# Stick-breaking weights by summation by parts: running products used as they are, values replaced by their steps along the sequence

## The chip, the cores and the metric

The program runs on one NeuronCore of a Trainium2 chip. Its matrix engine is TensorE (PE in the profile, with its weight loads shown apart as PEld), beside it work VectorE (DVE), ScalarE (ACT), GpSimd (POOL) and SyncE (SP), which issues nearly all transfers. The engines run side by side and meet at semaphores. The metric is the device time of one execution of the whole program in microseconds (us), as a median of several runs.

## The reference

Two layers on an input of 1024 rows by 1024 columns, float32: an attention layer and a recurrent layer, each followed by a dense SwiGLU block, with norms around every part. The change lies in the attention layer alone. It has 8 heads of ordinary chunked softmax attention (group A) and 8 heads of stick-breaking attention (group B), 64 columns each:

```
z = einsum('bqhd,bkhd->bhqk', q_blk, k) * scale
causal = kpos[None, :] < qpos[:, None]
log_beta = log_sigmoid(z)
log_1m_beta = where(causal, log_sigmoid(-z), 0.0)
after = cumsum(log_1m_beta, axis=3, reverse=True) - log_1m_beta
w = where(causal, exp(log_beta + after), 0.0)
o = einsum('bhqk,bkhd->bqhd', w, v)
```

Without logarithms: with s(k) = sigmoid(-z(k)) for k before the query and 1 from there on, and R(k) the product of s from k to the end, the weight of key k is w(k) = R(k+1) - R(k). The output is the sum of w(k) v(k) over the keys. Summation by parts turns it into the sum of (1 - R(k)) (v(k) - v(k-1)), with v(-1) = 0: the same number from other factors.

## The kernel before

The heads are worked in pairs, in the order 4, 5, 6, 7, 0, 1, 2, 3: first the four stick-breaking ("sigmoid") pairs, then the four softmax pairs. For each pair, `project` (L311) multiplies the normed input with the pair's query and key weights on PE (two query tiles and two key tiles `psq`, each 24 matmuls, in two PSUM banks `proj` that take turns), and ACT and DVE bring the results to SBUF as high and low parts `st` (L326 to L335). The values of two pairs at a time are computed by `v_tile` (L281, tiles `psv` in the same two banks) and brought to SBUF by `evacuate` (L298) as `v`, one tile [128, 8, 128] for each pair: partition p and block t hold key 128 t + p.

`attend` (L338) then takes the 8 query blocks of 128 rows one after the other, and the two heads of the pair in each. For a sigmoid pair, query block i has n = 128 (i + 1) keys, and for each head:

- PE makes the scores `sc` (L389, L390); ACT takes the sigmoid into `pr` (L397); POOL sets the entries from the diagonal on to 1 (L408), and column n to 1 (L407);
- DVE makes the running product R from the right, in place, by a scan (L411), and then the weights as the difference of neighbours, in place (L415); for the last block it also clears the last column (L417);
- PE transposes `pr` in blocks of 128 (L427) into one of two PSUM banks `tr`; ACT copies up to 512 columns at a time to SBUF as `pt` (L431);
- PE multiplies `pt` with `v` into `pso` (L356). These value matmuls are held back and run in bursts, for sigmoid pairs after blocks 3, 5, 6 and 7.

Four `pr` buffers take turns, so a sigmoid of a later block waits until the transposes of an earlier one have run. The weights' high and low parts and some other tiles share a ring of eight buffers "w" (`split`, L142 to L158).

The order on each engine is fixed when the program is built: a list scheduler places all instructions of all stages by estimated times. While a pair is attended, the projections and value tiles of the next pair are placed between its instructions, so PE has other matmuls (`psq`, `psv`) between scores and transposes.

Of the kernel before, what the change touches and what calls it, by code (L numbers as in the profile page):

```python
# [8 lines left out]
F32 = mybir.dt.float32  # L9
F32R = mybir.dt.float32r  # L10
BF16 = mybir.dt.bfloat16
AF = mybir.ActivationFunctionType
ALU = mybir.AluOpType
PSUM = bass.MemoryType.PSUM

P = 128
S = 1024
# [3 lines left out]
NT = S // P  # L21
# [78 lines left out]
class Trunk:  # L100
# [164 lines left out]
    def attention(self, x_src, xT_src, w_v, w_qk, bias_t, o_dst, hT, pools, open_first):  # L265
        nc, tc = self.nc, self.tc
        with ExitStack() as ctx:
# [6 lines left out]
            def turned_bank():  # L274
                return self.pt.tile([P, 512], F32, tag="tr", bufs=2, name=self.uid("tr"))
# [22 lines left out]
            def evacuate(vt, t2, both=False):  # L298
                psv = psvs.pop(t2)
                for tt in range(2):  # L300
# [4 lines left out]
                        nc.scalar.activation(vt[0][:, t, :], psv[:, tt, 0, :], AF.Copy, scale=rsc[:, t:t + 1])  # L305
                    nc.scalar.activation(vt[1][:, t, :], psv[:, tt, 1, :], AF.Copy, scale=rsc[:, t:t + 1])

            def v_alloc():
                return [ap.tile([P, NT, P], F32, tag="v", bufs=3, name=self.uid("v")) for _ in range(2)]

            def project(p, ws=(None, None)):  # L311
                st = [[ap.tile([P, S], F32R, tag="st", bufs=12, name=self.uid("st"))
                       for _ in range(3)] for _ in range(2)]
                for which in range(2):
                    w = ws[which] or self.split(w_qk[p, which], KT, P)
                    for half in range(2):
                        ps = prp.tile([P, 512], F32, tag="proj", bufs=2, name=self.uid("psq"))
                        self.proj_T(ps, w, slice(0, P), hT, half)
                        cs = slice(half * HALF, (half + 1) * HALF)
                        if which or p < 4:  # L320
                            nc.vector.tensor_tensor(ps, ps, rsb[:, cs], op=ALU.mult)
                        for h in range(2):
                            own, oth = (slice(0, 64), slice(64, P)) if h == 0 else (slice(64, P), slice(0, 64))
                            qs, k1, k2 = st[h]
                            if which == 0:
                                nc.scalar.activation(qs[own, cs], ps[own, :], AF.Copy, scale=-0.125)  # L326
                                nc.vector.scalar_tensor_tensor(
                                    qs[oth, cs], ps[own, :], -0.125, qs[own, cs].bitcast(F32),
                                    op0=ALU.mult, op1=ALU.subtract)
                            else:  # L330
                                nc.scalar.copy(k1[own, cs], ps[own, :])
                                nc.scalar.copy(k1[oth, cs], ps[own, :])
                                nc.vector.tensor_tensor(k2[own, cs], ps[own, :], k1[own, cs].bitcast(F32),
                                                        op=ALU.subtract)
                                nc.vector.tensor_copy(k2[oth, cs], k2[own, cs].bitcast(F32))  # L335
                return st

            def attend(p, st, vt):  # L338
                bias = [None, None]
# [25 lines left out]
                for i in range(NT):  # L365
                    k0 = max(0, i - 4) if p < 4 else 0
                    nb = i + 1 - k0
                    n = nb * P
# [4 lines left out]
                    w = n // n_c  # L373
                    for h in range(2):
                        qs, k1, k2 = st[h]
                        q = qs[:, i * P:(i + 1) * P]
                        if p < 4 and h == 1:
                            pr = ap.tile([P, 640], F32, tag="nata", bufs=3, name=self.uid("pr"))
                        else:
                            pr = ap.tile([P, 1024], F32, tag="nat", bufs=4, name=self.uid("pr"))  # L380
                        if p < 4:
                            mn = ap.tile([P, 2], F32, tag="mn", bufs=4, name=self.uid("mn"))
                            mn = [mn[:, c:c + 1] for c in range(n_c)]
                            sm = ap.tile([P, 1], F32, tag="sm", bufs=4, name=self.uid("sm"))
                        for c in range(n_c):
                            sc = pp.tile([P, 512], F32, tag="sc", bufs=3, name=self.uid("sc"))[:, :w]
                            ks = slice(k0 * P + c * w, k0 * P + c * w + w)
                            cs = slice(c * w, c * w + w)
                            nc.tensor.matmul(sc, q, k1[:, ks], start=True, stop=False)  # L389
                            scored = nc.tensor.matmul(sc, q, k2[:, ks], start=False, stop=True).ins  # L390
                            if p < 4:
                                off = 640 - n + c * w
                                nc.vector.tensor_tensor_reduce(
                                    pr[:, cs], sc, bias[h][:, off:off + w], 1.0, 3e38,
                                    op0=ALU.add, op1=ALU.min, accum_out=mn[c])
                            else:
                                nc.scalar.activation(pr[:, cs], sc, AF.Sigmoid, scale=rsc[:, i:i + 1])  # L397
                        if p < 4:
                            if n_c == 2:
                                nc.vector.tensor_tensor(mn[0], mn[0], mn[1], op=ALU.min)  # L400
                            nc.scalar.activation(pr[:, :n], pr[:, :n], AF.Exp, bias=mn[0], scale=-1.0,
                                                 accum_out=sm)
                            nc.vector.reciprocal(sm, sm)
                            nc.gpsimd.tensor_scalar(pr[:, :n], pr[:, :n], sm, 1.0, op0=ALU.mult, op1=ALU.mult)
                        else:
                            if n < S:
                                nc.gpsimd.memset(pr[:, n:n + 1], 1.0)  # L407
                            nc.gpsimd.affine_select(pr[:, n - P:n], pr[:, n - P:n], pattern=[[-1, P]],  # L408
                                                    compare_op=ALU.is_gt, fill=1.0, base=0,
                                                    channel_multiplier=1)  # L410
                            nc.vector.tensor_tensor_scan(  # L411
                                pr[:, 0:n][:, ::-1], pr[:, 0:n][:, ::-1], self.zero.to_broadcast([P, n]),
                                1.0, op0=ALU.mult, op1=ALU.add)
                            m = n if n < S else n - 1
                            nc.vector.tensor_tensor(pr[:, 0:m], pr[:, 1:m + 1], pr[:, 0:m], op=ALU.subtract)  # L415
                            if m < n:
                                nc.vector.memset(pr[:, m:n], 0.0)  # L417
                        nat.append(pr)
                    if p == seq[-1]:
                        self.scored.append(scored)  # L420
# [1 line left out]
                    for b0 in range(0, len(blocks), 4):  # L422
                        bl = blocks[b0:b0 + 4]
                        tr = turned_bank()
                        pt = ap.tile([P, 512], F32, tag="pt", bufs=7, name=self.uid("pt"))
                        for j, (kb, h) in enumerate(bl):
                            turned = nc.tensor.transpose(tr[:, j * P:(j + 1) * P],  # L427
                                                         nat[h][:, kb * P:(kb + 1) * P], self.ident).ins
                        w = len(bl) * P
                        if p >= 4 or (b0 // 4) % 2 == 0:  # L430
                            nc.scalar.copy(pt[:, :w], tr[:, :w])  # L431
                        else:
                            nc.vector.tensor_copy(pt[:, :w], tr[:, :w])
                        groups.append((i, nb, k0, bl, pt))
                        if not stretch:
                            values(groups, [])
                            groups = []
# [9 lines left out]
            vt = v_alloc()  # L447
# [89 lines left out]
            wk = self.split(None, KT, P, raw=wk)  # L537
            spread(1)
            st = project(seq[0], (wq, wk))
            for j, p in enumerate(seq):  # L540
                if j == 7:
                    prj.close()
                    pools[0] = open_first()
                attend(p, st, vt)
                if j < 7:
                    q = seq[j + 1]
                    if q % 2 == 0:
                        wv = v_weights(q // 2)
                        vt = v_alloc()
                        for t2 in range(4):  # L550
                            v_tile(q // 2, wv, vt, t2)
                            evacuate(vt, t2, q < 4)
                    st = project(q)


    def psum(self):
# [695 lines left out]
```

## Time and profile before

| what | number |
|---|---|
| median of 3 runs | 2197.12 us (2196.29 to 2198.2) |
| profiled execution, its own time | 2193.34 us |
| its span in the trace | 2191.5 us |
| mean granted TensorE clock | 0.998 |
| busy over the span | PE 99%, PEld 82%, DVE 70%, ACT 53%, POOL 10% |
| the attention's sigmoid pairs | about 57 to 305 us of the span |
| the softmax pairs | about 305 to 492 us |

The busy share is the time in which an engine has at least one instruction running. Matmuls are pipelined and overlap, so a PE that is shown as busy can still have small gaps between starts. "Idle before" names what an engine waited for before an instruction, inferred from semaphores; the chain of waits follows the last instruction back to whatever released each step. Times in the timeline count from the start of the span.

### The profile page before, as it was taken

The numbers are of one execution on the slowest core, as the hardware profiler recorded it, in microseconds if no ns is written. First come the engines' busy times: TensorE is split into PE (matmuls) and PEld (weight loads), VectorE is DVE, ScalarE is ACT, GpSimd is POOL, SyncE is SP. The second block draws the span as 40 slices with busy tenths as digits, with TensorE's granted clock in tenths as the row PEclk, the third lists the DMA queues.
The fourth block names the chain that finished last, engine by engine and source line by source line (L and its number), as shares of the span: only waits on it lengthen the run. The fifth ranks groups of instructions, "written<-read, shape, count | busy, mean of one in ns | idle before, by whom it ended". The sixth has DMA issues, their size and how long they took to land.

```text
span 2191.5 us, 30594 instructions
## 1 busy us (share of the span) xinstructions
PE 2159.3 (99%) x11140; PEld 1801.2 (82%) x11140; DVE 1542.0 (70%) x2526; ACT 1171.0 (53%) x2174; POOL 224.8 (10%) x450
## 2 busy tenths in 40 slices
PE   9999999999999999999999999999999999999998
PEld 8888889878788888888887777888788888888886
DVE  5877865656878776766767677437886777758675
ACT  6655555556855544433436676527755444424443
POOL 2111113121100000000001333102000000000011
PEclk9999999999999999999999999999999999999999
DMA  7101011127324333336468421356233333328565
GB/s 274 35 30 49 29 35 50 54 84 222 137 92 128 108 106 111 97 115 235 138 184 247 128 63 40 94 196 215 96 122 110 103 114 97 110 87 292 167 180 158
DMA packets 168278, 270.21 MB, mean 123 GB/s; under 512 B 13888, under 2 KB 94784, under 8 KB 168128
## 3 DMA queue, kind: packets, MB, share of 16 engines
q1 hardware_dynamic: 167488, 266.18, 38.0%
q10 hardware_dynamic: 640, 2.10, 0.3%
q8 instruction: 87, 1.43, 0.3%
q14 instruction: 63, 0.52, 0.1%
HBM read 202.69 MB, written 65.54 MB: 122 GB/s over the span
## 4 chain that ended last, share of the span: by engine, by line
PE 87%; DVE 5%; DMA 3%; issue 2%; ACT 2%; POOL 0%; SPq 0%; POOLq 0%; ACTq 0%; DVEq 0%
PE ps L743 13%; PE ps L742 13%; PE ps L744 13%; PE ps L585 7%; PE ps L827 5%; PE ps L829 5%; PE ps L828 5%; PE tr L427 3%; PE pso L356 3%; PE psq L166 2%; PE psq L167 2%; PE psq L168 2%; PE ps L167 2%; PE ps L166 2%; PE ps L168 2%
## 5 line engine op out<-in xcount | busy, mean ns | idle before, releaser
L743 PE MATMUL ps<-hS,q 128*128 128x512 f32 (+1 forms) x1288 | 489.4, 380 | 0.5 <-DVE hS L89 0.5
L742 PE MATMUL ps<-hS,q 128*128 128x512 f32 (+1 forms) x1288 | 489.6, 381 | 0.0
L744 PE MATMUL ps<-hS,q 128*128 128x512 f32 (+1 forms) x1288 | 488.8, 380 | 0.0
L713 DVE TENSOR_TENSOR q<-raw,q 128x512 fp32r<-128x512 f32 x308 | 205.4, 686 | 178.3 <-ACT q L712 177.7
L743 PEld LDWEIGHTS ps<-hS,q 128*128 128x128 f32 x1288 | 242.3, 188 | 46.8 <-DVE hS L89 0.9
L744 PEld LDWEIGHTS ps<-hS,q 128*128 128x128 f32 x1288 | 242.3, 188 | 45.9
L742 PEld LDWEIGHTS ps<-hS,q 128*128 128x128 f32 x1288 | 241.8, 188 | 46.3 <-DVE tf L89 0.2
L712 ACT CAST q<-raw 128x512 fp32r<-128x512 f32 x308 | 178.2, 616 | 169.7 <-DVE raw L721 118.1
L828 PE MATMUL ps<-o,o 128*128 128x512 f32 x616 | 240.2, 390 | 0.5 <-DVE o L823 0.5
L829 PE MATMUL ps<-o,o 128*128 128x512 f32 x616 | 238.1, 390 | 0.4 <-DVE o L957 0.4
L827 PE MATMUL ps<-o,o 128*128 128x512 f32 x616 | 221.6, 391 | 3.7 <-ACT o L956 2.9
L700 ACT ACTIVATE raw<-raw,gcol 128x256 f32<-128x256 f32 x352 | 150.4, 498 | 134.8 <-DMA raw<-in_ffn_w_up_dram 70.1
L822 ACT CAST o<-raw 128x512 fp32r<-128x512 f32 x184 | 110.5, 620 | 162.7 <-PE ps L829 60.1
L182 POOL TENSOR_SCALAR rs<-ss 128x1 f32<-128x1 f32 x52 | 28.6, 549 | 1420.5 <-ACT junk L178 1354.0
L823 DVE TENSOR_TENSOR o<-raw,o 128x512 fp32r<-128x512 f32 x184 | 123.4, 687 | 57.5 <-ACT o L822 56.8
L827 PEld LDWEIGHTS ps<-o,o 128*128 128x128 f32 x616 | 115.5, 188 | 30.7 <-ACT o L956 4.7
L828 PEld LDWEIGHTS ps<-o,o 128*128 128x128 f32 x616 | 115.7, 188 | 25.3 <-DVE o L823 1.6
L829 PEld LDWEIGHTS ps<-o,o 128*128 128x128 f32 x616 | 115.7, 188 | 24.9 <-DVE o L957 1.3
L156 DVE TENSOR_TENSOR wlo<-raw,whi 128x1024 fp32r<-128x1024 f32 x76 | 93.3, 1227 | 55.4 <-ACT whi L155 53.9
L411 DVE TENSOR_TENSOR_SCAN pr<-pr,zero 128x128 f32<-128x128 f32 (+7 forms) x64 | 86.9, 1361 | 30.7 <-POOL pr L408 25.7
L155 ACT CAST whi<-raw 128x1024 fp32r<-128x1024 f32 x76 | 79.7, 1050 | 45.8 <-PE ps L167 19.8
L166 PE MATMUL psq<-hT,whi 128*128 128x512 f32 x256 | 101.8, 398 | 0.1
(206 smaller groups left out, 4319.1 us busy)
## 6 DMA issues: line engine op xcount, KB each, us to landing
raw<-in_ffn_w_gate_dram SPq DMA_DIRECT2D x44, 512.0 KB, 4.2
raw<-in_ffn_w_up_dram SPq DMA_DIRECT2D x44, 512.0 KB, 4.2
gS<-c SPq DMA_DIRECT2D x88, 256.0 KB, 3.7
raw<-gS SPq DMA_DIRECT2D x88, 256.0 KB, 2.8
gA<-c SPq DMA_DIRECT2D x66, 256.0 KB, 3.5
raw<-in_ffn_w_down_dram SPq DMA_DIRECT2D x63, 256.0 KB, 4.6
raw<-gA SPq DMA_DIRECT2D x44, 256.0 KB, 2.9
t<-in_ffn_w_down_dram SPq DMA_DIRECT2D x22, 512.0 KB, 6.6
```

The costliest lines, as they stand in the source:

```text
L166: nc.tensor.matmul(ps, wh[:, kt, cols], hh[:, kt, :], start=kt == 0, stop=False)
L585: self.matmul = nc.tensor.matmul(ps[:, n * 512:(n + 1) * 512], x, y[:, n, :], start=first and i == 0, stop=last and i == len(passes) - 1).ins
L700: nc.scalar.activation(raw[:, i], raw[:, i], AF.Copy, scale=gain[:, 4 * k + i:4 * k + i + 1])
L712: self.last = nc.scalar.copy(t[:, 0], src).ins
L713: self.last_lo = nc.vector.tensor_tensor(t[:, 1], src, t[:, 0].bitcast(F32), op=ALU.subtract).ins
L742: nc.tensor.matmul(ps, a[:, 0, kt, :], bh, start=kt == 0, stop=False)
L743: nc.tensor.matmul(ps, a[:, 0, kt, :], bl, start=False, stop=False)
L744: self.matmul = nc.tensor.matmul(ps, a[:, 1, kt, :], bh, start=False, stop=kt == 3).ins
L823: tt(t[:, 1], src, t[:, 0].bitcast(F32), op=ALU.subtract)
L827: nc.tensor.matmul(ps, a[0], b[:, 0], start=first, stop=False)
L828: nc.tensor.matmul(ps, a[0], b[:, 1], start=False, stop=False)
L829: nc.tensor.matmul(ps, a[1], b[:, 0], start=False, stop=last)
```

## The change

Four edits in the attention layer.

1. For sigmoid pairs, `attend` no longer takes the difference of neighbours on DVE, no longer sets column n on POOL, and no longer clears the last column on DVE. `pr` holds R itself after the scan.
2. When ACT brings the transposed tile to SBUF, it computes 1 - R in the same instruction: an ACTIVATE (Copy with scale -1 and bias 1) in the place of a COPY.
3. A new function `steps` replaces both value tiles of two sigmoid pairs by v(k) - v(k-1). The preceding key lies on the partition before (or, for partition 0, on partition 127 of the block before), so `prev`, the tile shifted by one key, is filled by three transfers from SBUF to SBUF per tile (112, 15 and 1 partitions, the last one with 7 blocks of 128) and one POOL memset of the very first key's predecessor; DVE then subtracts in place. `steps` runs twice (for pairs 4 and 5, and for 6 and 7), so there are 12 transfers, 4 memsets and 4 subtractions of 128 by 1024. `prev` comes from the ring "w".
4. The DVE subtraction is placed behind the last key instruction of the projection that precedes it (`self.stacked`).

```diff
+            def steps(vt):
+                for v in vt:
+                    prev = self.main.tile([P, NT, P], F32, tag="w", bufs=8, name=self.uid("prev"))
+                    for r0, r1 in ((1, 113), (113, P)):
+                        nc.sync.dma_start(prev[r0:r1], v[r0 - 1:r1 - 1])
+                    nc.sync.dma_start(prev[0:1, 1:NT], v[P - 1:P, 0:NT - 1])
+                    nc.gpsimd.memset(prev[0:1, 0:1], 0.0)
+                    with self.behind([self.stacked]):
+                        nc.vector.tensor_tensor(v, v, prev, op=ALU.subtract)
...
-                                nc.vector.tensor_copy(k2[oth, cs], k2[own, cs].bitcast(F32))
+                                self.stacked = nc.vector.tensor_copy(k2[oth, cs], k2[own, cs].bitcast(F32)).ins
...
-                            if n < S:
-                                nc.gpsimd.memset(pr[:, n:n + 1], 1.0)
...
-                            m = n if n < S else n - 1
-                            nc.vector.tensor_tensor(pr[:, 0:m], pr[:, 1:m + 1], pr[:, 0:m], op=ALU.subtract)
-                            if m < n:
-                                nc.vector.memset(pr[:, m:n], 0.0)
...
-                        if p >= 4 or (b0 // 4) % 2 == 0:
+                        if p >= 4:
+                            nc.scalar.activation(pt[:, :w], tr[:, :w], AF.Copy, bias=1.0, scale=-1.0)
+                        elif (b0 // 4) % 2 == 0:
...
             st = project(seq[0], (wq, wk))
+            steps(vt)
...
                     st = project(q)
+                    if q == 6:
+                        steps(vt)
```

The scheduler places everything anew, so the order on all engines moves within the attention. Two places on DVE, with buffer numbers kept (L419 is the scan that was L411, L331 to L345 are the former L321 to L335, L316 is the new subtraction; the scan is listed under the name SCALAR_TENSOR_TENSOR). The first is the end of pair 4, its query blocks 5 and 6, with the last key tile of pair 5 between them. Before:

```order
L411 SCALAR_TENSOR_TENSOR pr101_874<-pr101_874,zero_70 128x768
L321 TENSOR_TENSOR psq154_1189<-psq154_1189,rsb_182 128x512
L156 TENSOR_TENSOR wlo264_1942<-raw262_1939,whi263_1941 128x1024
L415 TENSOR_TENSOR pr101_874<-pr101_874 128x768
L411 SCALAR_TENSOR_TENSOR pr110_932<-pr110_932,zero_70 128x896
L333 TENSOR_TENSOR st141_1081<-psq154_1189,st140_1080 64x512
L415 TENSOR_TENSOR pr110_932<-pr110_932 128x896
L335 CAST st141_1081<-st141_1081 64x512
L411 SCALAR_TENSOR_TENSOR pr113_947<-pr113_947,zero_70 128x896
L333 TENSOR_TENSOR st144_1084<-psq154_1189,st143_1083 64x512
```

And with the change, on the same engine at the same place:

```order
L419 SCALAR_TENSOR_TENSOR pr103_864<-pr103_864,zero_70 128x768
L331 TENSOR_TENSOR psq156_1169<-psq156_1169,rsb_182 128x512
L419 SCALAR_TENSOR_TENSOR pr112_920<-pr112_920,zero_70 128x896
L156 TENSOR_TENSOR wlo266_1890<-raw264_1887,whi265_1889 128x1024
L343 TENSOR_TENSOR st143_1061<-psq156_1169,st142_1060 64x512
L345 CAST st143_1061<-st143_1061 64x512
L419 SCALAR_TENSOR_TENSOR pr115_933<-pr115_933,zero_70 128x896
L343 TENSOR_TENSOR st146_1064<-psq156_1169,st145_1063 64x512
```

The differences (L415) are gone from between the scans and the key tile's instructions, and the weight split L156 has moved behind a scan. The second place is the start of pair 4, between its own last key tile and the first query tile of pair 5 (`psq148`, in the new program `psq150`). Before:

```order
L335 CAST st50_532<-st50_532 64x512
L411 SCALAR_TENSOR_TENSOR pr62_687<-pr62_687,zero_70 128x256
L415 TENSOR_TENSOR pr58_671<-pr58_671 128x128
L415 TENSOR_TENSOR pr62_687<-pr62_687 128x256
L411 SCALAR_TENSOR_TENSOR pr64_698<-pr64_698,zero_70 128x256
L327 SCALAR_TENSOR_TENSOR st139_1079<-psq148_1091,st139_1079 64x512
L415 TENSOR_TENSOR pr64_698<-pr64_698 128x256
L411 SCALAR_TENSOR_TENSOR pr68_716<-pr68_716,zero_70 128x384
L327 SCALAR_TENSOR_TENSOR st142_1082<-psq148_1091,st142_1082 64x512
```

And with the change:

```order
L345 CAST st50_532<-st50_532 64x512
L316 TENSOR_TENSOR v5_115<-v5_115,prev55_659 128x1024
L316 TENSOR_TENSOR v6_116<-v6_116,prev56_665 128x1024
L419 SCALAR_TENSOR_TENSOR pr64_695<-pr64_695,zero_70 128x256
L419 SCALAR_TENSOR_TENSOR pr66_704<-pr66_704,zero_70 128x256
L337 SCALAR_TENSOR_TENSOR st141_1059<-psq150_1071,st141_1059 64x512
L419 SCALAR_TENSOR_TENSOR pr70_720<-pr70_720,zero_70 128x384
L156 TENSOR_TENSOR wlo246_1600<-raw244_1597,whi245_1599 128x1024
L419 SCALAR_TENSOR_TENSOR pr72_729<-pr72_729,zero_70 128x384
L337 SCALAR_TENSOR_TENSOR st144_1062<-psq150_1071,st144_1062 64x512
```

The two step subtractions now stand ahead of the scans of query block 1, and a weight split (L156) and a second scan stand ahead of the L337 that empties the first query tile. On PE and ACT the instructions of the sigmoid pairs are the same in number but for edit 2; the `psv` and `psq` matmuls that lie between them have shifted places by some tens of instructions.

## Prediction

> **What bounds the kernel now.** I read the page first: how full PE is, and what the chain of waits consists of.
>
> ```profile
> span 2191.5 us, 30594 instructions
> PE 2159.3 (99%) x11140; PEld 1801.2 (82%) x11140; DVE 1542.0 (70%) x2526; ACT 1171.0 (53%) x2174; POOL 224.8 (10%) x450
> PE 87%; DVE 5%; DMA 3%; issue 2%; ACT 2%; POOL 0%; SPq 0%; POOLq 0%; ACTq 0%; DVEq 0%
> ```
>
> PE is the bound: 2159.3 us of 2191.5, and 87% of the chain. The change takes nothing from PE; it takes work from DVE. It can only pay where PE waits for DVE. So the next view is the busy time by stretch, for the sigmoid pairs (57 to 305 us) and the softmax pairs behind them; the columns are PE, PEld, DVE, ACT, POOL, granted clock, DMA share and GB/s.
>
> ```profile
> 57.00:305.00 248.00, 243.12 (x1853) 214.45 (x1852) 188.50 (x229) 144.62 (x281) 35.73 (x120) 1.00 0.11 36
> 305.00:446.00 141.00, 141.00 (x1037) 125.21 (x1036) 86.12 (x269) 78.07 (x170) 34.30 (x56) 1.00 0.16 51
> ```
>
> In the sigmoid pairs PE idles 248.00 - 243.12 = 4.9 us; behind them it doesn't idle until 446 us, in code that the change leaves as it is. The granted clock is 1.00 throughout. PE's timeline, in brackets the idle before and what ended it, says where the 4.9 us lie.
>
> ```profile
> 102.37 0.39 PE L291 MATMUL psv<-whi,hT 128*128 128x256 f32 x1 [1.51 <-DVE st L333]
> ...
> 123.84 0.55 PE L427 MATMUL tr<-ident,pr 128*128 128x128 f32 x3 [1.00 <-DVE pr L415]
> ...
> 225.38 0.55 PE L427 MATMUL tr<-ident,pr 128*128 128x128 f32 x3 [1.07 <-DVE pr L415]
> ...
> 245.11 0.55 PE L427 MATMUL tr<-ident,pr 128*128 128x128 f32 x3 [1.05 <-DVE pr L415]
> ```
>
> All four end with DVE: 1.51 + 1.00 + 1.07 + 1.05 = 4.63 us. They sit at the ends of pairs 4 and 6 and the starts of 5 and 7, where the scans are long or `pr` buffers come free late. Three wait for a difference (L415) itself, the first for a key tile that DVE empties behind scans and differences.
>
> An idle counts from the modelled end of the matmul before. These two rows show that an end isn't a cost:
>
> ```profile
> 76.13 0.39 PE L166 MATMUL psq<-hT,whi 128*128 128x512 f32 x1
> 76.36 0.40 PE L167 MATMUL psq<-hT,whi 128*128 128x512 f32 x1
> ```
>
> A matmul lasts 0.39 us, but the next starts 0.23 us after it. So each real stop costs about 0.39 - 0.23 = 0.16 us more than its idle: the four cost 1.67 + 1.16 + 1.23 + 1.21 = 5.27 us.
>
> **What the change removes.** The groups by shape:
>
> ```profile
> L415 DVE TENSOR_TENSOR pr<-pr 128x128 f32<-128x128 f32 (+7 forms) x64 | 48.0, 755 | 1.5
> L407 POOL MEMSET pr<- 128x1 f32 x56 | 5.3, 98 | 81.4 <-PE tr L427 79.8 <-DVE pr L411 1.3
> ```
>
> 64 differences, 48.0 us, and 8 memsets of one column leave DVE; 56 memsets, 5.3 us, leave POOL (busy 35.73 of 248 us, so worth nothing by itself). Of the 48 us, nearly all lie beside PE work: PE is stopped for only 5.27 us in all. How much of each stop goes is read from the chain of waits: the differences that lie on it ahead of each stop.
>
> ```profile
> by line: DVE pr L411 40.4%; DVE st L333 12.8%; DVE pr L415 12.3%; DVE wlo L156 12.2%; issue 7.9%; PE psv L291 7.4%; PE psv L293 4.8%; PE psv L292 4.8%; DVE st L335 4.2%
> ```
>
> ```profile
> by line: DVE pr L411 41.5%; PE tr L427 18.6%; DVE pr L415 17.4%; issue 6.0%; POOL pr L408 3.6%; PE psv L292 3.0%; PE psv L291 2.9%; PE psv L293 2.9%; PE sc L389 2.2%; PE sc L390 2.2%; POOL pr L407 1.4%; POOLq L408 0.6%
> ```
>
> ```profile
> 221.17 1.09 DVE pr L415
> ...
> 224.23 1.10 DVE pr L415
> ```
>
> ```profile
> by line: DVE pr L411 40.7%; PE tr L427 24.2%; DVE pr L415 17.4%; issue 6.1%; PE sc L390 4.0%; POOL pr L408 3.6%; PE psv L291 2.6%; PE sc L389 1.8%; POOL pr L407 1.4%; POOLq L408 0.6%
> ```
>
> The windows of the first, second and fourth answer are 94 to 104, 117 to 125 and 238 to 246 us. Ahead of the first stop the differences on the chain are 12.3% of 10 us = 1.23 us, ahead of the second and fourth 17.4% of 8 us = 1.39 us each, ahead of the third 1.09 + 1.10 = 2.19 us. Each stop shrinks by the smaller of its cost and of what goes ahead of it: 1.23 of 1.67, 1.16 of 1.16, 1.23 of 1.23, 1.21 of 1.21. The sum is 4.83 us. What is late next there is PE itself, or the border between pairs: the first sigmoid of a pair needs a `pr` buffer that the last transposes of the pair before set free. That path runs through PE, ACT and POOL, holds no difference, and stays.
>
> **What it adds.** 4 subtractions of 128 by 1024 on DVE, the ACTIVATEs in the place of copies, 12 transfers and 4 small memsets. Nearest rows by shape:
>
> ```profile
> L415 DVE TENSOR_TENSOR pr<-pr 128x1023 f32<-128x1023 f32 x8 | 9.8, 1224 | 0.3
> ...
> L431 ACT COPY pt<-tr 128x512 f32<-128x512 f32 x92 | 52.7, 589 | 40.4 <-PE tr L427 39.6
> ...
> L326 ACT ACTIVATE st<-psq 64x512 fp32r<-64x512 f32 x32 | 19.0, 593 | 22.8 <-DVE st L327 19.7 <-DVE psq L321 2.7 <-PE psq L168 0.3
> ...
> L397 ACT ACTIVATE pr<-sc,small 128x512 f32<-128x512 f32 x24 | 16.3, 697 | 12.3 <-PE tr L427 6.7 <-PE sc L390 5.6
> ```
>
> The subtractions take 4 x 1.224 = 4.9 us of DVE. The new evacuation is an ACTIVATE with a fixed scale: nearest is L326, 593 ns against 589 ns for the copy, so 80 of them (20 for each pair) add 0.3 us; at most it is L397, which reads its scale from a column, 697 ns and 8.6 us in all. Less than zero is excluded, since it reads and writes the same. ACT is busy 144.62 of 248 us in this stretch, and either end hides there; I take 0 on the path, and if the cover failed, 0.1 us for each transpose group that waits for its bank.
>
> The transfers have to come between the last value evacuation and the subtraction. For pairs 4 and 6, from ACT's timeline, and then the casts on DVE behind which the subtractions are placed:
>
> ```profile
> 39.63 0.36 ACT L306 ACTIVATE v<-psv,small 128x128 f32<-128x128 f32 x1
> ...
> 147.22 0.42 ACT L306 ACTIVATE v<-psv,small 128x128 f32<-128x128 f32 x1
> ```
>
> ```profile
> 64.57 0.42 DVE L335 CAST st<-st 64x512 fp32r<-64x512 f32 x1
> ...
> 183.74 0.42 DVE L335 CAST st<-st 64x512 fp32r<-64x512 f32 x1
> ```
>
> For pair 4 the values are ready at 40.0 us and the cast ends at 65.0: 25 us. For pair 6 they are ready at 147.6 and the cast ends at 184.2: 37 us. The trace has no transfer from SBUF to SBUF; the bounds are the quickest and the slowest of the DMA view:
>
> ```profile
> oT<-ob SPq DMA_DIRECT2D x16, 256.0 KB, 2.0
> ...
> gcol<-in_gcol_dram SPq DMA_DIRECT2D x1, 12.0 KB, 10.6
> ```
>
> 2.0 to 10.6 us, against 25 and 37: I take 0, and no row gives a gain. Behind the transfers on SP's queue stand weights of a pair that is worked one or two pairs later (pair 6 in the first case, pair 0 in the second), so a start up to 10 us later costs 0 as well. POOL's 4 memsets take the place of 56.
>
> What isn't hidden by so much is the start of pair 4 on DVE. There two subtractions and one weight split (L156, of the same 128 by 1024) come ahead of the second L327 of pair 5's first query tile, and the scans of blocks 1 and 2 with them. That L327 today:
>
> ```profile
> 68.95 0.69 DVE L327 SCALAR_TENSOR_TENSOR st<-psq,st 64x512 fp32r<-64x512 f32 x1
> ```
>
> The L327 ends at 69.64; with 3 x 1.224 = 3.7 us more in front of it, at most 73.3. PE needs that bank again for the next key tile, which starts at 76.13 (row above). So 2.8 us remain, and I take 0; the scans that start 3.7 us late have caught up by block 3, since blocks 0 to 3 lose as much in differences. The upper bound is 3.7 us at pair 4 and as much at pair 6, where the same pieces come together.
>
> **The sum.** 2193.34 (profiled execution) - 4.83 + 0 = 2188.5 us for a profiled execution. The median of the runs, 2197.12, is 3.8 us above the profiled execution, and it is the median that is compared: 2197.12 - 4.83 = **2192.3 us**. A measurement of this kernel can tell about 0.2% from no change, that is 4.4 us, so the forecast lies just beyond it.
>
> **The rivals.**
>
> *Off the path (B).* PE is full, and the work that DVE loses was beside it. For it: 243.12 of 248 us, and a scheduler that places the fillers anew can set new stops of the same size, at the pair borders, where ACT and POOL come last. Against it: three of the four waits name the removed line itself. It gives 2197.1 less, say, one of the four stops (1.2 us): 2196. The Trainium skill ("Perfetto Trace Analysis", § Identifying the Most-Contended Engine) says to optimize the engine with the highest occupancy first; here that is PE, and by that rule alone the time would stay where it is. This trace agrees on which engine that is (99% against 70%), while the four waits show DVE on the path in places.
>
> *More goes than the four stops (C).* The chain runs on DVE around each stop, and with the differences gone the transposes of blocks 5 to 7 come early enough for the fillers to spread. All 5.27 us go, and the idle of the weight loads ahead of the transposes with them:
>
> ```profile
> L427 PEld LDWEIGHTS tr<-ident,pr 128*128 128x128 f32 x528 | 62.3, 141 | 16.3 <-issue 5.7 <-DVE pr L415 3.9 <-ACT pt L431 0.7
> ```
>
> 3.9 - (1.00 + 1.07 + 1.05) = 0.8 us more by L415, and some 2 us of the 5.7 that the profile calls issue: about 8 us, 2189.
>
> *The steps in the way (D).* The late DVE work at the start of pairs 4 and 6 delays the scans, PE runs out of filler, and the ends of these pairs come as much later as the differences would have saved. Price 2 x 3.7 = 7.4 us: 2204.5, slower. It decides if PE needs the bank of pair 5's first query tile less than 3.7 us after today's L327 ends; today it is 76.13 - 69.64 = 6.5 us, which speaks against it.
>
> **How the numbers follow.** Forecast A 0.50 (2190 to 2194.5), B 0.27, C 0.15, D 0.08. A lies on both sides of the bound of 4.4 us (2192.7): I count 0.35 of its 0.50 as faster. Faster: 0.35 + 0.15 = 0.50. Same: 0.15 + 0.27 = 0.42. Slower: 0.08. The range takes in A, B and C with 2 us for their own spread: 2187 to 2197.5; D is left out.
>
> **What would show it.** Right: no wait of PE for L415's successor at the ends of pairs 4 and 6, PE idle in the sigmoid stretch under 1.5 us, DVE busy there near 188.5 - 43.6 = 145 us, the new ACTIVATE near 593 ns, the subtractions without a wait for a transfer. Wrong: PE idle as large as before with ACT or POOL as releasers (B); DVE waiting for `prev`, or PE for L337 around 73 to 77 us (D); a sigmoid stretch shorter by over 6 us (C).

## The result and the profile after

The changed kernel ran at 2190.37 us (median of 6 runs, 2186.95 to 2191.27), the kernel before beside it at 2197.88 us: ratio 0.9963, 95% interval [0.9952, 0.9974], so 7.5 us faster. The forecast was 4.8 us. Two more comparisons of the same pair of kernels follow below; they gave 0.9975 and 0.9988, so that the size needs a better ruler than the median.

First the sigmoid pairs in the changed kernel, busy time by stretch, with the columns as before (PE, PEld, DVE, ACT, POOL, clock, DMA share, GB/s):

```profile
57.00:305.00 248.00, 247.32 (x1874) 218.36 (x1873) 151.98 (x169) 146.51 (x285) 28.76 (x70) 1.00 0.14 44
```

PE idles 248.00 - 247.32 = 0.7 us where it idled 4.9. DVE went from 188.50 to 151.98 us, ACT stayed. The view of waits, PE's alone in this stretch, is all that is left of the idle time (what waited, for whom, us in total, times, longest):

```profile
PE sc L399 <- ACT pr L407: 0.5, 2, 0.2
PE psq L166 <- DVE st L337: 0.2, 1, 0.2
```

The four stops that ended with DVE are gone. Of what was added, the second row is the only trace on PE: L337 is the old L327 at the start of pair 4, the one place that the prediction called tight. The added work itself, from the groups (the DVE rows of this stretch alone) and from the DMA issues (KB of each, median us to landing):

```profile
L419 DVE TENSOR_TENSOR_SCAN pr<-pr,zero 128x128 f32<-128x128 f32 (+7 forms) x64 | 86.6, 1358 | 51.3 <-POOL pr L416 49.6
...
L316 DVE TENSOR_TENSOR v<-v,prev 128x1024 f32<-128x1024 f32 x4 | 4.8, 1245 | 0.1
...
L435 ACT ACTIVATE pt<-tr 128x512 f32<-128x512 f32 x64 | 36.9, 600 | 29.6 <-PE tr L431 29.3
...
prev<-v SPq DMA_DIRECT2D x4, 448.0 KB, 4.3
prev<-v SPq DMA_DIRECT2D x4, 60.0 KB, 3.8
prev<-v SPq DMA_DIRECT2D x4, 3.5 KB, 2.6
```

The subtractions (L316) cost 1245 ns each and stood idle for 0.1 us in all, so no transfer was late. The new ACTIVATE takes 600 ns against the copy's 589. The scans' row shows how DVE's place has changed: its idle time ahead of a scan is now 51.3 us, and nearly all of it is POOL's fill of the diagonal block, behind ACT's sigmoid. DVE waits for the others, and PE for none of them.

**A ruler with less scatter.** The matmuls of the first output projection (L585 in the kernel before, L594 in the changed one) start near the end of the softmax pairs, behind all that the change touches; from there on both kernels run the same code. In PE's timeline, for the kernel before, the same kernel in a second run, the changed kernel in a second run and in a third:

```profile
453.57 0.40 PE L585 MATMUL ps<-whi,first 128*128 128x512 f32 x1
```

```profile
454.79 0.40 PE L585 MATMUL ps<-whi,first 128*128 128x512 f32 x1
```

```profile
449.31 0.63 PE L594 MATMUL ps<-whi,first 128*128 128x512 f32 x1
```

```profile
448.04 0.40 PE L594 MATMUL ps<-whi,first 128*128 128x512 f32 x1
```

The same program differs by 1.2 to 1.35 us here, and one row goes with it. In the opening, 10 to 20 us, the granted clock of the kernel before is 1.00 in the trace shown with the prediction and 0.83 in its second run:

```profile
10.00:20.00 10.00, 8.89 (x69) 8.49 (x70) 8.41 (x20) 10.00 (x24) 1.44 (x4) 1.00 1.02 408
```

```profile
10.00:20.00 10.00, 8.76 (x58) 8.33 (x58) 8.57 (x20) 10.00 (x24) 1.29 (x4) 0.83 1.02 410
```

The lag is there before the sigmoid pairs begin: their first scores start at 57.6 us in the one and at 58.8 in the other. The changed kernel opened at 0.83 in its first two traces (first output projection at 449.39 and 449.31) and 1.00 in the third. Compared at equal clock, the change gains 454.79 - 449.31 = 5.48 us at 0.83 and 453.57 - 448.04 = 5.53 us at 1.00. The two traces that came with the result differ by only 4.2 us since one opened at 1.00 and the other at 0.83.

The ruler moves by up to half a microsecond of its own. In the slice 440 to 450 us the granted clock was 0.95 and 0.96 in the first two traces of the changed kernel, 0.86 in the run without the steps and 0.93 in the run without the difference (both below), and 1.00 in all others. The last long burst of value matmuls ahead of that mark (L356, in the changed kernel L366) starts at 447.46 and 448.68 us in the two traces of before, and at 441.92 and 443.18 in the third and second of the changed kernel: 5.54 us at 1.00 and 5.50 at 0.83, the same gain.

Behind the first projection, the way to the end took 1737.9 us in the trace of before and between 1733.3 and 1739.3 us in the others (1743.4 to 1744.2 in three that ran together, where the kernel before took 2201.21 us), all of it the same code: that scatter of several us is what the medians carry.

### The profile page after: what moved, and what is told of

Read it like the earlier page. It is cut to its first block, busy times and chain, and to the rows that moved or that the text cites. A ratio compares the mean times of both kernels' runs of the same rounds, so it can differ in the third digit from the quotient of the medians.

```text
span 2188.7 us, 30464 instructions
## 1 busy us (share of the span) xinstructions
PE 2160.6 (99%) x11140; PEld 1803.1 (82%) x11140; DVE 1502.0 (69%) x2458; ACT 1171.6 (54%) x2174; POOL 210.3 (10%) x398
## 4 chain that ended last, share of the span: by engine, by line
PE 88%; DVE 4%; DMA 3%; ACT 2%; issue 2%; POOL 0%; SPq 0%; POOLq 0%; ACTq 0%; DVEq 0%
PE ps L752 13%; PE ps L753 13%; PE ps L751 13%; PE ps L594 7%; PE ps L837 5%; PE ps L838 5%; PE ps L836 5%; PE pso L366 3%; PE tr L431 3%; PE psq L166 3%; PE psq L167 2%; PE psq L168 2%; PE ps L166 2%; PE ps L167 2%; PE ps L168 2%
## 5 line engine op out<-in xcount | busy, mean ns | idle before, releaser
L156 DVE TENSOR_TENSOR wlo<-raw,whi 128x1024 fp32r<-128x1024 f32 x76 | 93.6, 1231 | 57.4 <-ACT whi L155 56.3
L419 DVE TENSOR_TENSOR_SCAN pr<-pr,zero 128x128 f32<-128x128 f32 (+7 forms) x64 | 86.6, 1358 | 51.3 <-POOL pr L416 49.6
L155 ACT CAST whi<-raw 128x1024 fp32r<-128x1024 f32 x76 | 79.7, 1049 | 48.5 <-PE ps L167 19.9
```

## The experiments

The table has all of them; "first projection" is the start of the first output projection, "against" the kernel before at the same clock of the opening (453.57 at 1.00, 454.79 at 0.83), in us.

| kernel | clock 10:20 | first projection | against | ratio of the runs, 95% interval |
|---|---|---|---|---|
| before, again | 0.83 | 454.79 | | 0.9994 [0.9986, 1.0003] |
| after, again | 0.83 | 449.31 | -5.48 | 0.9975 [0.9966, 0.9985] |
| after, third time | 1.00 | 448.04 | -5.53 | 0.9988 [0.9976, 1.0000] |
| after without the steps | 1.00 | 448.46 | -5.11 | 0.9981 [0.9972, 0.9990] |
| before without the difference | 0.83 | 449.57 | -5.22 | 0.9988 [0.9979, 0.9998] |
| before with the steps on top | 1.00 | 453.64 | +0.07 | 0.9998 [0.9989, 1.0007] |
| before without it in pairs 4, 6 | 0.83 | 451.59 | -3.20 | 0.9994 [0.9984, 1.0004] |
| before without it in pairs 5, 7 | 1.00 | 449.84 | -3.73 | 0.9977 [0.9966, 0.9987] |
| before, a copy behind each difference | 1.00 | 456.15 | +2.58 | 1.0014 [1.0005, 1.0023] |
| before, difference on GpSimd | 0.83 | 457.83 | +3.04 | 1.0006 [0.9997, 1.0015] |
| after, idle load, free | (0.61) | 465.40 | | 1.0044 [1.0031, 1.0056] |
| after, idle load, held | 0.83 | 456.02 | +1.23 | 1.0009 [0.9996, 1.0021] |

**Both kernels again.** No edit.

> The kernel before once more, nothing changed. Both theories: the same time within 0.2% (2193 to 2199 us). Its profile says how the profiled execution lies against the timed runs: if the 7.5 us between the medians are real and the 4.2 us between the two traces are only the luck of one execution, this trace should have its first output projection (L585) later than 453.57 us and a span above 2191.5 us.

> The changed kernel once more, nothing changed. Faster by 4 to 8 us (ratio 0.9965 +- 0.002). If the gain lies wholly in the attention stage, its first output projection (L594) starts 4 to 8 us ahead of that of the kernel before on the same chip, with the rest of the program as long in both.

Measured: as the section above has it, 5.48 us at the first projection. The expected sign that the first trace of before had been a quick one came true, 1.2 us of it by the opening's clock; the span, though, was shorter by 0.9 us. A third comparison was made last:

> The changed kernel once more, to settle the size: the first comparison gave 7.5 us, the second 5.4, and the first output projection of their traces came 5.5 us earlier where the opening ran at the same clock (454.79 against 449.31). Theory 'the gain is what the attention stage gains, the rest is scatter of the stages behind it': ratio between 0.9965 and 0.9985, and the first output projection (L594) at 449.3 us with a granted clock of 0.83 in the slice 10 to 20 us, or near 448.2 with 1.00 there. Rival 'something behind the attention gains 2 us too': ratio below 0.9968, with a shorter way from the first output projection to the end.

Its first projection lay at 448.04 us with a clock of 1.00, as expected. The ratio of the runs, 0.9988, missed the expected 0.9965 to 0.9985 on the small side. The three ratios 0.9963, 0.9975 and 0.9988 average 0.9975, or 5.4 us; that agrees with the gain of the attention, and nothing behind it is needed. The 7.5 us of the first comparison lie at the high end of this scatter.

**The steps alone: taken out of the changed kernel, and put on top of the kernel before.** In the first, the sigmoid pairs multiply 1 - R by the unstepped values; in the second, they take both differences.

```
-            steps(vt)
...
-                    if q == 6:
-                        steps(vt)
```

> The changed kernel without the steps: no shifting transfers and no four subtractions, so the sigmoid pairs multiply the running products by the values themselves (that part of the output is left wrong). Theory 'the steps are off the path' (what the prediction said): the same time as the changed kernel within 1.5 us, 7 us under the kernel before. Rival 'the steps are in the way': up to 7 us faster than the changed kernel, ratio to before about 0.993.

> The kernel before with the steps added and the differences kept: all that the change adds but the evacuation, and nothing of what it takes away (the sigmoid pairs' output is left wrong, since a difference is taken twice). Theory 'the steps are off the path': the time before within 1 us. Rival 'the steps are in the way': 2 to 7 us slower, with TensorE waiting near 73 to 76 us, at the start of pair 4.

Measured: without the steps the first projection comes at 448.46 (with them 448.04, both at 1.00); with the steps on top of before it comes at 453.64 (without 453.57, both at 1.00). The steps cost nothing that can be seen at the end of the attention. (The 0.4 us by which the run without them is later lie in the slower clock just ahead of the mark, 0.86 as given above: the value burst before it starts at 441.90 us without the steps and at 441.92 with them.) The second kernel shows how: PE does stop at the start of pair 4, just where the rival had placed it. Its stops in the stretch 70 to 80 us of PE's timeline:

```profile
71.91 0.55 PE L437 MATMUL tr<-ident,pr 128*128 128x128 f32 x3 [0.80 <-DVE pr L425]
73.19 0.47 PE L166 MATMUL psq<-hT,whi 128*128 128x512 f32 x1 [0.73 <-DVE st L337]
```

That is 1.53 us of idle. But the stop of 1.51 us behind L333, at 102.37 in the kernel before, is missing from this kernel's waits. So is the third of the four, at 225.38. New stops took the place of old ones: up to the first projection PE's idle time is 0.86 us shorter than before (453.64 - 443.63 against 453.57 - 442.70) and the shown time of its matmuls 0.93 us longer, and the end didn't move. In the changed kernel there is no such stop to lose, and at 73.85 us only 0.18 us is left of the first:

```profile
73.85 0.50 PE L166 MATMUL psq<-hT,whi 128*128 128x512 f32 x1 [0.18 <-DVE st L337]
```

**The removal alone.** The kernel before, with L407, L415 and L417 struck out (the difference is left out, nothing replaces it).

```
-                            nc.vector.tensor_tensor(pr[:, 0:m], pr[:, 1:m + 1], pr[:, 0:m], op=ALU.subtract)
```

> The kernel before with the differences, and the two small fills that belong to them, left out, and nothing put in their place: the sigmoid pairs' output is left wrong, no steps, and the evacuation of the turned bank stays the COPY. Theory 'the removal is the whole gain': the same as the changed kernel within 1.5 us, 5 to 8 us under the kernel before. Rival 'the evacuation or the small fills count': more than 2 us from the changed kernel.

```profile
449.57 0.63 PE L579 MATMUL ps<-whi,first 128*128 128x512 f32 x1
```

5.22 us earlier than before at 0.83, against 5.48 for the whole change: the removal is the gain. (At the value burst, ahead of the slower clock, it is 448.68 - 442.79 = 5.89 us against 5.50; what the change adds and the new order together cost no more than 0.4.) The ratio of the runs says 2.6 us, [0.4, 4.6], smaller than the trace. Of the table's intervals this one and the third of the changed kernel's miss what the first projection shows, by 0.6 and 0.3 us, and that of the first comparison by 0.2 on the other side; why the stages behind fell out so was not followed up.

**Where the gain sits: differences out of two pairs at a time** (in the two others they stay; the sigmoid pairs without them are left without the difference).

```
+                            if p in (5, 7):
                                 nc.vector.tensor_tensor(pr[:, 0:m], pr[:, 1:m + 1], pr[:, 0:m], op=ALU.subtract)
```

> The kernel before with the differences left out of pairs 4 and 6 alone, in whose values and transposes the four stops lie (102, 124, 225 and 245 us); pairs 5 and 7 keep theirs (the output of pairs 4 and 6 is left wrong). Theory 'four stops': the whole gain, 4.5 to 5.5 us: first output projection at 449 to 450 us. Rival 'the gain is spread over all 64 rows': half of it, 2.7 us, first output projection near 452.

> The kernel before with the differences left out of pairs 5 and 7 alone, where the trace of before shows no stop over 0.5 us (the output of pairs 5 and 7 is left wrong). Theory 'four stops': no gain, first output projection at 453.5 to 455 us, time within 1 us of before. Rival 'spread over all rows': half the gain, near 452.

These lines show a misreading of mine: two of the four stops, at 123.84 and 245.11 us, stand in the first transposes of pairs 5 and 7, as the prediction had said ("the starts of 5 and 7"), and I put them into pairs 4 and 6. PE's waits for DVE in the sigmoid stretch, without the differences of 4 and 6, and then without those of 5 and 7:

```profile
PE tr L428 <- DVE pr L416: 2.0, 2, 1.0
```

```profile
PE psv L291 <- DVE st L333: 1.5, 1, 1.5
```

The first kernel keeps the two stops of pairs 5 and 7 and loses the other two: by the prediction's prices 1.67 + 1.23 = 2.90 us, measured 3.20. The second keeps only the first stop and loses three: 1.16 + 1.23 + 1.21 = 3.60, measured 3.73. A gain spread evenly over 64 rows would be 2.7 and 2.7 and would add up to 5.5; these add up to 6.9, since the stop at 225 us is lost in both. The gain follows the stops that go, within 0.3 us, and not the number of rows. That the stop in pair 6 goes although pair 6 keeps its differences was not expected. The order of PE's work is drawn anew for each kernel, and I have no run with the old order held, so whether DVE's shorter queue or the new order removes it stays open.

**More on the chain.** A copy of each row onto itself, behind the difference.

```
+                            nc.vector.tensor_copy(pr[:, 0:m], pr[:, 0:m])
```

> The kernel before with a copy of the row onto itself on VectorE behind each difference, so that the chain is longer by about as much again as the change took out (0.1 to 1.1 us a row). Theory 'a few waits, each cut by what the chain loses': the four stops that stood at 1.0 to 1.5 us grow by about the length of the copy, and more waits of the same kind open: slower by more than the 5 to 7.5 us which the removal gained, since no wait can shrink below nothing but every wait can grow; I expect +10 to +25 us. Rival 'the waits were set by something else': the same time within 3 us.

The copies took 28.9 us of DVE, 459 ns each, and the first projection came 2.58 us later: far under the 10 to 25 that I expected. The theory's second half falls, that every wait can grow. PE's waits in the sigmoid stretch:

```profile
PE tr L428 <- DVE pr L416: 3.3, 3, 1.3
PE tr L428 <- DVE pr L418: 1.8, 2, 1.4
PE psv L291 <- DVE st L333: 0.8, 1, 0.8
PE sc L389 <- ACT pr L397: 0.7, 2, 0.6
```

They are still the ends and starts of pairs (L418 is the cleared column of the last block), six of DVE's in place of four, none over 1.5 us. Everywhere else the longer chain on DVE made no stop.

**The load away, the chain kept.** The same difference on GpSimd.

```
-                            nc.vector.tensor_tensor(pr[:, 0:m], pr[:, 1:m + 1], pr[:, 0:m], op=ALU.subtract)
+                            nc.gpsimd.tensor_tensor(pr[:, 0:m], pr[:, 1:m + 1], pr[:, 0:m], op=ALU.subtract)
```

> The kernel before with the difference on GpSimd in place of VectorE: VectorE loses the 36 us, but the chain from scan to transposes keeps a difference, and a longer one (I estimate twice as long, from the mean of GpSimd's own pass over the same rows), with a hop between engines. Theory 'the length of the chain': slower than before, by 5 us or more. Rival 'VectorE's load': faster than before by 4 us or more, as the changed kernel.

Slower, by 3.0 us at the first projection (expected 5 or more; the ratio of the runs, 1.0006 [0.9997, 1.0015], doesn't tell it from no change), though DVE is busy for only 152.67 us of the stretch, the same as in the changed kernel. PE's one long stop now ends with POOL, and the clock falls in the slices around it:

```profile
117.67 0.57 PE L427 MATMUL tr<-ident,pr 128*128 128x128 f32 x3 [3.10 <-POOL pr L407]
```

```profile
110.00:120.00 10.00, 6.89 (x81) 6.26 (x79) 4.31 (x6) 3.16 (x8) 5.36 (x9) 0.90 0.01 2
120.00:130.00 10.00, 9.48 (x88) 7.82 (x85) 4.78 (x4) 6.95 (x18) 4.82 (x12) 0.93 0.07 27
```

So taking work off DVE doesn't pay by itself, and "VectorE's load" falls as a full account. What the lighter load alone is worth can't be read from this run, since the longer chain on POOL works against it.

**The load back, the chain short.** The changed kernel with a maximum over n zeros on DVE for each scan, on which nothing depends. In the first try nothing held it in its place.

```
+                            nc.vector.tensor_reduce(idle, self.zero.to_broadcast([P, n]), axis=mybir.AxisListType.X, op=ALU.max)
```

> The changed kernel with a maximum over n zeros on VectorE behind each of the 64 scans (about 0.1 to 1.1 us each), on which nothing depends: VectorE's load of the removed differences comes back, but the transposes wait only for the scan. Theory 'the length of the chain scan, difference, transposes': the same time as the changed kernel within 1.5 us, and no stop of TensorE over 0.5 us in the sigmoid stretch. Rival 'VectorE's load': 4 to 8 us slower than the changed kernel, about the time before, with VectorE's busy time in the stretch back near 188 us and the four stops back.

The try missed its aim. From the groups of DVE in the first 57 us, and from the busy time:

```profile
L423 DVE TENSOR_REDUCE sm<-zero 128x1 f32<-128x128 f32 (+7 forms) x50 | 33.3, 723 | 0.1
```

```profile
10.00:20.00 10.00, 5.47 (x26) 4.76 (x27) 10.00 (x20) 10.00 (x24) 1.80 (x1) 0.61 1.02 409
```

Since they depend on nothing, 50 of the 64 stood in the opening, where PE waits for DVE's weight splits and norms: PE fell to 5.47 us of 10, the clock to 0.61, and the first projection came at 465.40. It says that the opening has no room on DVE, and nothing on the sigmoid pairs. In the second try the same instruction is issued behind its scan:

```
+                            with self.behind([scan]):
+                                nc.vector.tensor_reduce(idle, self.zero.to_broadcast([P, n]),
+                                                        axis=mybir.AxisListType.X, op=ALU.max)
```

> The changed kernel with the same idle maximum over n zeros behind each of the 64 scans, but now held to issue behind its scan, so that it stands in the sigmoid stretch and not in the opening. VectorE gets some 46 us back (64 of 723 ns) and the transposes still wait only for the scan. Theory 'the length of the chain': the first output projection (L594 in the changed kernel) starts within 1.5 us of the changed kernel's 449.3. Rival 'VectorE's load': at about the time of the kernel before, 453.5 to 455, with waits of TensorE for VectorE of 4 us or more back in the stretch.

```profile
57.00:305.00 248.00, 244.79 (x1846) 214.40 (x1845) 186.78 (x221) 142.85 (x274) 30.96 (x66) 0.99 0.13 41
70.00:80.00 10.00, 8.06 (x33) 6.14 (x32) 9.81 (x13) 4.93 (x8) 1.66 (x2) 0.83 0.37 106
```

```profile
PE tr L435 <- DVE pr L419: 1.3, 1, 1.3
PE psv L291 <- DVE st L343: 0.7, 1, 0.7
PE psq L166 <- DVE st L337: 0.6, 1, 0.6
```

First projection at 456.02, 6.7 us later than the changed kernel: the theory, as I wrote it, said 1.5 at most and falls too. The rival comes nearer in time, not in the waits: 2.6 us of waits for DVE, not 4, and other ones than the four. The 1.3 and the 0.6 lie at the start of pair 4, where the two subtractions already stand, and there the clock falls to 0.83 for a slice, by estimate worth 10 x 0.17 = 1.7 us. Up to the first projection, against the second run of the changed kernel, PE's idle time is 3.3 us longer (456.02 - 446.10 = 9.92 against 449.31 - 442.67 = 6.64) and the shown time of its matmuls 3.4 us longer; the slow slice is about half of the latter, and the rest I can't place.

Read together with GpSimd's run, "chain" and "load" were a false choice. DVE works in its given order, and the idle maximum of one head stands in front of the scan of the other, whose transposes PE needs as well. It is on the chain without any dependency. What counts is how late DVE delivers the few rows that PE has no filler for: moving the difference to another engine doesn't bring them sooner, and putting other work in DVE's queue makes them late again.

## Why the prediction was right, and what it mis-sized

- **PE is bound, and DVE pays only where PE stops.** Right: the stretch's idle time fell from 4.9 to 0.7 us, and the runs without the differences in two pairs each give the price of the stops they lose. The Trainium skill ("Perfetto Trace Analysis", § Identifying the Most-Contended Engine) says to optimize the most-contended engine first, the one with the highest occupancy (for TensorE it goes by the share of peak flops or by the weight loads). This trace agrees on which engine that is: PE with 99%, its weight loads with 82%, DVE with 70%. That the time would then stay where it is was the prediction's own reading, not the section's, and it did not hold: 48 us taken from an engine that is 70% busy gave 5.5, since PE's stops ended with it.
- **The size, 4.83 us, against 5.5.** The mechanism was right, and the term for the first stop too small. It was taken at 1.23 us in place of 1.67, by the share of differences in the chain of waits ahead of it; the stop went entirely, which is 0.44 of the missing 0.7. DVE's own rows in the kernel before show what the share left out:

```profile
94.52 1.05 DVE L415 TENSOR_TENSOR pr<-pr 128x768 f32<-128x768 f32 x1
...
98.01 1.07 DVE L415 TENSOR_TENSOR pr<-pr 128x896 f32<-128x896 f32 x1
...
101.62 0.69 DVE L333 TENSOR_TENSOR st<-psq,st 64x512 fp32r<-64x512 f32 x1
```

Two differences of 1.05 and 1.07 us stand in front of the L333 that PE waits for. The chain counts 0.22 + 1.01 us of them and puts 0.66 us beside the first down to "issue". With 2.12 us in place of 1.23, the prediction's own rule lets the stop go whole, and its sum is 5.27. In the third run of the changed kernel, whose opening ran at the same clock, this instruction (now L343) ends at 99.74 us in place of 102.31; PE comes to the value tile at 101.71, where before it had stood ready from 100.86. So DVE is 2.57 us earlier, and PE, in its new order, 0.85 later. Where the rest lies, PE's rows up to the first projection show, before and after, both with an opening at 1.00:

```profile
0.00:453.57 453.57, 442.70 (x3262) 391.62 (x3263) 312.11 (x579) 267.61 (x544) 81.91 (x213) 1.00 0.21 74
```

```profile
0.00:448.04 448.04, 441.45 (x3263) 391.40 (x3264) 270.69 (x511) 267.56 (x544) 73.54 (x161) 1.00 0.23 79
```

Idle time fell from 10.87 to 6.59, by 4.28 us; another 1.25 us left the matmuls' own shown time. The prediction counted 4 x 0.16 = 0.64 us of that kind, for starts held back inside the span of the matmul before. In the pair of traces that opened at 0.83 it is 0.76 us (443.43 against 442.67), and idle time fell by 4.72. So 0.1 to 0.6 us more than counted left the shown time; at which starts isn't shown.
- **DVE's busy time: 145 us forecast, 151.98 found.** The 43.6 us that it took off are 48.0 of differences and 0.5 of fills, less 4.9 of subtractions. But rows on DVE overlap at their ends (the difference at 94.52 above ends at 95.57, the scan behind it starts at 95.49): the groups of the stretch add up to 194.4 us before, where DVE is busy for 188.50, and to 154.4 after, against 151.98. So 3.5 of the 7 us had never counted as busy time. The other 3.5 came into the window, which is fixed while PE is further along in it: one weight split more (1.2 us), and more of the key, query and softmax work.
- **The additions at 0.** Right at the end of the attention (with and without them -0.4 to +0.1 us at the first projection, 0.0 to 0.1 at the value burst), but not for the reason given. At the start of pair 4, 2.8 us were to remain until PE needs the bank at 76.13 us. That time was no fixed mark: in PE's new order the matmul that needs the bank stood at 73.85 (72.60 in the third run), with a wait of 0.18 us for L337. With the differences still in, PE stopped there for 1.53 us in all, and two of the old stops went. The ACTIVATE at 600 ns was costed between 593 and 697; the transfers landed in 1.7 to 4.7 us, inside the 2.0 to 10.6 but for the shortest (the quickest row of the view was 1.8 us, for 4 KB, and not the 2.0 that the prediction calls so). One cost was not named: a weight's high part on ACT (L155) waited 3.7 us in two times for the subtraction to free its slot of the ring "w"; ACT had that room.
- **The rivals.** B (fillers placed anew set new stops) did not happen here, though it did in the runs with the load put back. C spoke of 8 us: the first median of 7.5 looks like it, but its own sign, a sigmoid stretch shorter by over 6 us, did not come, and the later comparisons give 5.4. D's mechanism is real and its price of 7.4 us was not: 0.18 us of wait in the changed kernel, and 1.53 in the run with the differences still in, whose end came 0.07 us later.
- **"Faster" as a coin toss.** The gain lay near what a comparison can tell (4.4 us by the prediction's measure): one of three intervals touches 1.0000.

## What to carry to other kernels

Where one engine is full, price work taken from another only at the full engine's stops, and read what stands ahead of a stop in the rows of the engine it waits for, since the shares of the chain can hide part of it; here all four stops went whole. Measure a change of a few us at a mark in the trace right behind the changed stage, at equal granted clock: identical code behind it scattered by 6 us, as much as the gain of 5.5. An instruction on which nothing depends isn't free on an engine that works in order, and one without a tie to its place may be scheduled where it hurts most.

## What the runs showed of the hardware

The granted clock can fall where PE stops, but not every time. A lone stop of 3.10 us came with 0.90 and 0.93 in two slices (table of GpSimd's run), and idle time of 1.94 us within 70 to 80 us with 0.83 in that slice, while 1.53 us of idle in the same place left it at 1.00. By estimate that is 1.7 us in the slices of each of the first two (10 x 0.10 + 10 x 0.07, and 10 x 0.17). One and the same stop, of about 1.65 us ahead of the last scores of the attention, came with 0.83 in the slice 450 to 460 in both traces of before, and with 1.00 up to 460 us in the third run of the changed kernel. What decides it no run here shows.

DVE was slower beside GpSimd's passes over the rows. DVE's groups in the sigmoid stretch, with the difference on GpSimd, and in the second run of the kernel before:

```profile
L411 DVE TENSOR_TENSOR_SCAN pr<-pr,zero 128x128 f32<-128x128 f32 (+7 forms) x64 | 90.7, 1425 | 52.8 <-POOL pr L408 47.6 <-POOL pr L407 3.8
...
L335 DVE CAST st<-st 64x512 fp32r<-64x512 f32 x17 | 11.7, 690 | 0.6
```

```profile
L411 DVE TENSOR_TENSOR_SCAN pr<-pr,zero 128x128 f32<-128x128 f32 (+7 forms) x64 | 86.9, 1361 | 30.7 <-POOL pr L408 25.7 <-PE tr L427 2.6 <-POOL pr L407 1.8
...
L335 DVE CAST st<-st 64x512 fp32r<-64x512 f32 x18 | 7.7, 426 | 0.6
```

The scan grew by 5%, the cast from 426 to 690 ns in the mean. Taken one by one in DVE's timeline, six of the 17 casts took 1.04 to 1.41 us, all six beside a difference on GpSimd; the ten with none beside them took 0.42 each, and so did one that had. The same difference took 1267 ns on GpSimd against 756 on DVE. And a shift by one partition from SBUF to SBUF, 448 KB in 112 rows, landed in 4.3 us in the median.
